# RoPE on one core: splitting the first load around the small inputs, and issuing half of the stores from GpSimd

## Chip, cores, metric

One core of a Trainium2 chip. The metric is the device time of one execution in microseconds (us). The kernel before takes 85.66 us (median of three runs, 85.59 to 85.97).

## The reference

```python
x: float32 (8, 8, 1024, 64); freqs: (32,); positions: int (1024,); scale = 0.5
angles = np.outer(positions * scale, freqs)
cos, sin = np.cos(angles), np.sin(angles)
x_first, x_second = x[..., :32], x[..., 32:]
out = concat([x_first * cos - x_second * sin,
              x_first * sin + x_second * cos], axis=-1).astype(np.float32)
```

16.8 MB are read and 16.8 MB are written.

## The kernel before

The data is cut into eight units of 2 MB, each 128 partitions of 16 KB. Unit 0 is loaded as it is by SyncE and cast to half precision on ScalarE. Units 1 to 7 are loaded by GpSimd, whose transfers cast on the way. VectorE builds the angles from positions and frequencies, ScalarE takes sine and cosine. Then each unit takes four VectorE instructions, a cast back on ScalarE, and a store.

```python
BUF_O = 4
...
    X0f = xin.tile([P, N], FP32, name="X0f")
    nc.sync.dma_start(out=X0f, in_=xv[0])
    pos_i64 = consts.tile([HP, K], positions.dtype)
    nc.scalar.dma_start(out=pos_i64, in_=positions.rearrange("(q k) -> q k", k=K))
    freq_row = consts.tile([1, half], FP32)
    nc.scalar.dma_start(out=freq_row, in_=freqs[None, :])
    ...
    load(1)                       # nc.gpsimd.dma_start(out=X[u], in_=xv[u]), casts
    ...
    for u in range(2, NU):
        load(u)
    ...                           # angles, sinT, cosT; ScalarE casts X0f into X[0]
    for u in (1, 0, *range(2, NU)):
        ps = prods.tile([P, K, 2, half], FP16, tag="ps")
        pin(nc.vector.tensor_tensor(out=ps, in0=X[u], in1=sin_b, op=ALU.mult))
        pin(nc.vector.tensor_tensor(out=X[u], in0=X[u], in1=cos_b, op=ALU.mult))
        ...                       # subtract into the first halves, add into the second
        OUT = xout.tile([P, N], FP32, tag="O")      # four buffers
        pin(nc.scalar.copy(out=OUT, in_=X[u].rearrange("p k h j -> p (k h j)")))
        nc.sync.dma_start(out=ov[u], in_=OUT)
```

## Time and profile before

| | kernel before |
|---|---|
| median time, span of the profiled run | 85.66 us, 83.9 us |
| frequencies land, first rotation starts | 7.82, 17.19 us |
| last store issued, landed on its last DMA engine | 76.43, 82.68 us |
| from the last landing to the end of the span | 1.20 us |
| busy: VectorE, ScalarE | 62.6, 37.4 us |

The span is shorter than the time by a constant 1.8 us; differences can be compared. "Landing" is the arrival of a completion record; a large transfer here runs on 16 DMA engines, each of which leaves one, and the last of them counts. The lines of the page, of the chain of waits and of the windows that carry the argument are in the prediction. "The hole" below is the short stretch, around 77 us, in which the DMA engines have finished the seventh store and the last one has only just been issued.

### The profile page before, as it was taken

What the parts mean: (1) busy time and instruction counts of PE and PEld (TensorE: products, weight loads), DVE (VectorE), ACT (ScalarE), POOL (GpSimd) and SP (SyncE); (2) the same over time, 40 slices, a digit from 0 to 9 for tenths busy, and PEclk for the clock granted to TensorE, in tenths of its full rate; (3) what the DMA queues carried; (4) which work ended last, traced back from release to release, by engine and by line L of the source; (5) the groups of instructions that cost most, each with busy time, mean ns of one, the idle gap of its engine ahead of it and who ended that gap; (6) DMA issues with size and microseconds to landing.
All of it is one profiled execution on the core that took longest, in us unless ns stands there. A gap on an engine that the chain in (4) does not pass through costs nothing.

```text
span 83.9 us, 151 instructions
## 1 busy us (share of the span) xinstructions
PE 1.1 (1%) x4; PEld 0.9 (1%) x4; DVE 62.6 (75%) x40; ACT 37.4 (45%) x12; POOL 4.5 (5%) x13
## 2 busy tenths in 40 slices
PE   0002300000000000000000000000000000000000
PEld 0002200000000000000000000000000000000000
DVE  0010699889999999999999999999999999600000
ACT  1400000799749309608905921950880591294000
POOL 5960000000000000000000000000000000000000
DMA  3599999999999999999999999999999999998890
GB/s 78 207 402 328 289 207 219 215 211 223 203 230 203 231 191 238 313 336 305 313 348 324 313 313 277 426 438 438 438 430 414 445 414 430 438 430 375 375 500 0
DMA packets 2338, 26.22 MB, mean 313 GB/s; under 512 B 274, under 2 KB 290, under 8 KB 290
## 3 DMA queue, kind: packets, MB, share of 16 engines
q1 hardware_dynamic: 1296, 18.87, 53.6%
q0 software_dynamic: 1008, 7.34, 42.7%
q10 hardware_dynamic: 34, 0.01, 0.2%
HBM read 16.79 MB, written 16.78 MB: 400 GB/s over the span
## 4 chain that ended last, share of the span: by engine, by line
DVE 72%; DMA 8%; ACT 7%; DVEq 1%; PE 1%; issue 1%; ACTq 1%
DVE X L136 22%; DVE ps L135 21%; DVE X L137 12%; DVE X L140 9%; DMA freq_row<-in_freqs_dram 8%; ACT OUT L144 4%; DVE r L116 3%; DVE y L107 3%; ACT sinT L120 2%; DVE m L114 1%; DVEq L176 1%; PE cfreq L92 1%; PE pos_ps L100 1%; ACTq L64 0%; DVE posf L104 0%
## 5 line engine op out<-in xcount | busy, mean ns | idle before, releaser
L144 ACT CAST OUT<-X 128x4096 f32<-128x4096 f16 x8 | 28.8, 3605 | 25.0 <-DVE X L140 25.0
L135 DVE TENSOR_TENSOR ps<-X,sinT 128x4096 f16<-128x4096 f16 x8 | 18.3, 2284 | 0.7 <-ACT sinT L120 0.7
L136 DVE TENSOR_TENSOR X<-X,cosT 128x4096 f16<-128x4096 f16 x8 | 18.3, 2292 | 0.3
L137 DVE TENSOR_TENSOR X<-X,ps 128x2048 f16<-128x2048 f16 x8 | 9.8, 1224 | 0.3
L140 DVE TENSOR_TENSOR X<-ps,X 128x2048 f16<-128x2048 f16 x8 | 9.7, 1217 | 0.0
L120 ACT ACTIVATE sinT<-r 128x2048 f16<-128x2048 f32 x1 | 1.9, 1910 | 12.2 <-DVE r L116 12.2
L71 POOL DMA_DIRECT2D X<-in_x_dram x7 | 3.9, 567 | 0.8 <-POOLq L162 0.8
L127 ACT CAST X<-X0f 128x4096 f16<-128x4096 f32 x1 | 3.6, 3587 | 0.0
L104 DVE COPY posf<-pos_ps 128x64 f32<-128x64 f32 x1 | 0.2, 225 | 4.0 <-PE pos_ps L100 4.0
L95 DVE CAST pos_row<-pos_i 16x64 f32<-16x64 int32 x1 | 0.2, 241 | 3.9 <-DMA pos_i<-in_positions_dram 3.9
L116 DVE SCALAR_TENSOR_TENSOR r<-m,y 128x2048 f32<-128x2048 f32 x1 | 2.3, 2292 | 0.0
L107 DVE TENSOR_TENSOR y<-posf,cfreq 128x2048 f32<-128x2048 f32 x1 | 2.3, 2286 | 0.0
L120 ACT ACT_TABLE_LOAD x1 | 1.3, 1283 | 1.7 <-issue 1.7
L126 ACT ACTIVATE cosT<-ra,quarter 128x2048 f16<-128x2048 f32 x1 | 2.0, 1985 | 0.0
L114 DVE TENSOR_SCALAR m<-y 128x2048 f32<-128x2048 f32 x1 | 1.2, 1227 | 0.0
L122 DVE TENSOR_SCALAR ra<-r 128x2048 int32<-128x2048 int32 x1 | 1.2, 1226 | 0.0
L88 DVE MEMSET coef<- 1x128 f32 x1 | 0.2, 165 | 0.8 <-PEq L162 0.8
L92 PE MATMUL cfreq<-freq_row,coef 1*128 1x32 f32 x2 | 0.6, 392 | 8.0 <-DMA freq_row<-in_freqs_dram 8.0
L100 PE MATMUL pos_ps<-pos_row,sel 16*128 16x64 f32 x2 | 0.7, 432 | 0.0
L92 PEld LDWEIGHTS cfreq<-freq_row,coef 1*128 1x128 f32 x2 | 0.5, 308 | 7.9 <-issue 7.9
L100 PEld LDWEIGHTS pos_ps<-pos_row,sel 16*128 16x128 f32 x2 | 0.5, 328 | 0.0
L77 POOL TENSOR_SCALAR_AFFINE_SELECT sel<-sel 16x128 f32<-16x128 f32 x1 | 0.3, 332 | 0.1
(6 smaller groups left out, 0.7 us busy)
## 6 DMA issues: line engine op xcount, KB each, us to landing
out_dram<-OUT SPq DMA_DIRECT2D x8, 2048.0 KB, 14.3
X<-in_x_dram POOLq DMA_DIRECT2D x7, 1024.0 KB, 24.5
X0f<-in_x_dram SPq DMA_DIRECT2D x1, 2048.0 KB, 10.2
pos_i<-in_positions_dram ACTq DMA_DIRECT2D x1, 8.0 KB, 4.1
freq_row<-in_freqs_dram ACTq DMA_DIRECT2D x1, 0.1 KB
```

The source lines that it names most:

```text
L71: nc.gpsimd.dma_start(out=X[u].rearrange("p k h j -> p (k h j)"), in_=xv[u])
L100: nc.tensor.matmul(out=pos_ps, lhsT=sel.rearrange("q a b -> q (a b)"), rhs=pos_row, start=True, stop=True)
L107: pin(nc.vector.tensor_tensor(out=y, in0=posf.unsqueeze(2).broadcast_to((P, K, half)), in1=cfreq.unsqueeze(1).broadcast_to((P, K, half)), ...
L114: pin(nc.vector.tensor_scalar(out=m, in0=y, scalar1=_MAGIC, scalar2=None, op0=ALU.add))
L116: pin(nc.vector.scalar_tensor_tensor(out=r, in0=m, scalar=_MAGIC, in1=y, op0=ALU.subtract, op1=ALU.subtract))
L120: pin(nc.scalar.activation(out=sinT, in_=r, func=AF.Sin, bias=0.0, scale=-_TWO_PI_DN))
L127: pin(nc.scalar.copy(out=X[0].rearrange("p k h j -> p (k h j)"), in_=X0f))
L135: pin(nc.vector.tensor_tensor(out=ps, in0=X[u], in1=sin_b, op=ALU.mult))
L136: pin(nc.vector.tensor_tensor(out=X[u], in0=X[u], in1=cos_b, op=ALU.mult))
L137: pin(nc.vector.tensor_tensor(out=X[u][:, :, 0, :], in0=X[u][:, :, 0, :], in1=ps[:, :, 1, :], op=ALU.subtract))
L140: pin(nc.vector.tensor_tensor(out=X[u][:, :, 1, :], in0=ps[:, :, 0, :], in1=X[u][:, :, 1, :], op=ALU.add))
L144: pin(nc.scalar.copy(out=OUT, in_=X[u].rearrange("p k h j -> p (k h j)")))
```

## The change

Its intent: to have the frequencies sooner, so that VectorE starts sooner; and to let the loads run first, by putting the first four stores into the same queue behind them.

```diff
-    nc.sync.dma_start(out=X0f, in_=xv[0])
+    pin = tc.keep_in_program_order
+    nc.sync.dma_start(out=X0f[:, : N // 2], in_=xv[0][:, : N // 2])
...
-    nc.scalar.dma_start(out=pos_i64, ...)
+    pin(nc.scalar.dma_start(out=pos_i64, ...))
-    nc.scalar.dma_start(out=freq_row, in_=freqs[None, :])
+    pin(nc.scalar.dma_start(out=freq_row, in_=freqs[None, :]))
+    pin(nc.scalar.dma_start(out=X0f[:, N // 2 :], in_=xv[0][:, N // 2 :]))
...
-    for u in (1, 0, *range(2, NU)):
+    for i, u in enumerate((1, 2, 0, *range(3, NU))):
...
-        nc.sync.dma_start(out=ov[u], in_=OUT)
+        (nc.gpsimd if i < NU // 2 else nc.sync).dma_start(out=ov[u], in_=OUT)
```

More of the change, by code (lines that the diff above doesn't have):

```diff
@@ L60 @@
     X0f = xin.tile([P, N], FP32, name="X0f")
-    nc.sync.dma_start(out=X0f, in_=xv[0])
+    pin = tc.keep_in_program_order
+    nc.sync.dma_start(out=X0f[:, : N // 2], in_=xv[0][:, : N // 2])
     pos_i64 = consts.tile([HP, K], positions.dtype)
-    nc.scalar.dma_start(out=pos_i64, in_=positions.rearrange("(q k) -> q k", k=K))
+    pin(nc.scalar.dma_start(out=pos_i64, in_=positions.rearrange("(q k) -> q k", k=K)))
     freq_row = consts.tile([1, half], FP32)
-    nc.scalar.dma_start(out=freq_row, in_=freqs[None, :])
+    pin(nc.scalar.dma_start(out=freq_row, in_=freqs[None, :]))
+    pin(nc.scalar.dma_start(out=X0f[:, N // 2 :], in_=xv[0][:, N // 2 :]))
     X = [xin.tile([P, K, 2, half], FP16, name=f"X{u}") for u in range(NU)]
@@ L82 @@
         load(u)
-    pin = tc.keep_in_program_order
     coef = consts.tile([1, P], FP32)
```

## The prediction

> **What bounds the kernel now.** I read the page first, for who is busy and what the chain of waits says. The chain ends in VectorE work:
>
> ```profile
> DVE 72%; DMA 8%; ACT 7%; DVEq 1%; PE 1%; issue 1%; ACTq 1%
> ```
>
> In order of time, the chain (the second view; columns are start, length, what) has these joints:
>
> ```profile
> 1.19 6.64 DMA freq_row<-in_freqs_dram
> ...
> 7.96 0.60 PE cfreq L92 x2
> 8.56 0.49 PE pos_ps L100 x2
> ...
> 9.08 0.23 DVE posf L104
> ...
> 17.19 2.30 DVE ps L135
> ...
> 72.80 3.60 ACT OUT L144
> ```
>
> So the 128-byte frequency row holds everything up until 7.82 us. From there to the first rotation is fixed work: 17.19 - 7.82 = 9.37 us. Then eight units of 6.92 us on VectorE (17.19 to 24.19, 31.11 and so on, no gap), a 3.60 us cast, and the last store is issued at 76.43. This view alone says: bring the frequencies earlier, and the end comes earlier by as much.
>
> The page's rows of forty slices say otherwise:
>
> ```profile
> DVE  0010699889999999999999999999999999600000
> ...
> DMA  3599999999999999999999999999999999998890
> ...
> HBM read 16.79 MB, written 16.78 MB: 400 GB/s over the span
> ```
>
> DMA is at 90% or more from the third slice almost to the end, longer than VectorE is. The third view, busy time by window, with DMA share and GB/s in the last two columns, tells whether this is real saturation:
>
> ```profile
> 0.00:1.70 1.70, 0.00 (x0) 0.00 (x0) 0.17 (x2) 0.00 (x0) 0.68 (x5) 1.00 0.00 0
> 1.70:3.70 2.00, 0.00 (x0) 0.00 (x0) 0.00 (x0) 1.28 (x1) 1.91 (x6) 1.00 0.85 233
> 3.70:5.70 2.00, 0.00 (x0) 0.00 (x0) 0.24 (x1) 0.00 (x0) 1.93 (x4) 1.00 0.99 418
> 20.00:28.00 8.00, 0.00 (x0) 0.00 (x0) 7.93 (x5) 6.15 (x2) 0.00 (x0) 1.00 1.04 217
> 34.50:54.00 19.50, 0.00 (x0) 0.00 (x0) 19.33 (x12) 9.56 (x4) 0.00 (x0) 1.00 1.02 325
> 56.00:76.00 20.00, 0.00 (x0) 0.00 (x0) 16.55 (x11) 10.41 (x3) 0.00 (x0) 1.00 1.01 433
> 76.00:77.50 1.50, 0.00 (x0) 0.00 (x0) 0.00 (x0) 0.41 (x1) 0.00 (x0) 1.00 0.82 350
> 77.50:78.50 1.00, 0.00 (x0) 0.00 (x0) 0.00 (x0) 0.00 (x0) 0.00 (x0) 1.00 0.77 328
> 78.50:82.40 3.90, 0.00 (x0) 0.00 (x0) 0.00 (x0) 0.00 (x0) 0.00 (x0) 1.00 0.92 387
> 82.40:83.90 1.50, 0.00 (x0) 0.00 (x0) 0.00 (x0) 0.00 (x0) 0.00 (x0) 1.00 0.00 0
> ```
>
> GB/s counts bytes at the destination, and a casting load writes half of what it reads: 217 is 434 GB/s of reading. The mixed stretch at 325 is half 434 of writing and half 217. The rate is thus one and the same, about 433 GB/s, for loads, stores and both. All 33.57 MB at 433 GB/s take 77.5 us of the 83.9 us span. What is left is 1.7 us before the first packet, about 0.9 us lost in 1.70 to 3.70 (233 instead of 418 for 2 us), the weak second around 77 to 78, and 1.2 us after the last landing.
>
> The records of landings settle it. The last engine's parts of stores 3 to 7 land at 63.00, 67.88, 72.72, 77.56 and 82.68 us: 4.88, 4.84, 4.84 and 5.12 apart, while the casts come 6.92 apart. Stores were queued up and drained at DMA speed. Only the last, issued at 76.43 just before the sixth had drained, found a small hole: 5.12 - 4.86 = 0.26 us. The kernel is bound by the DMA engines, and the VectorE chain has nearly caught up with them at the very end. The chain of waits names VectorE only because it follows the last store's own release.
>
> **What the Trainium skill says.** "DMA: Bandwidth & Descriptors", section "Where 436 GB/s comes from", gives 435 GB/s for the ports of the 16 engines, and says that between HBM and SBUF about 358 binds instead. This trace shows 433 in one direction, so here the first figure is the limit. The same page, "Issuing engines are not separate DMA queues", says that it doesn't matter to the transfer which engine issues it. The trace agrees for loads: mixed pairs of a GpSimd load and a SyncE store take 9.8 us, like two stores. Its "Queues, rings and completion order" says each DMA engine takes turns among queues, packet by packet. That agrees too (after 32 us loads and stores alternate), but a newcomer waits longer than one turn: store 0 was issued at 27.93 and its packets begin at about 31.8, and the frequency packet, issued at 1.19, moves at 6.25. "SBUF — State Buffer", section "Who interferes with whom", warns that VectorE can keep GpSimd from writing descriptors only in its two-port modes, not in tensor_tensor. During the stores VectorE runs only tensor_tensor, so I expect no harm; the trace of before has no GpSimd issue at that time to show it.
>
> **The change part by part.** No byte and no engine instruction is added or removed; one load becomes two.
>
> *Half of unit 0 behind the frequencies.* Ahead of the frequency packet there are now 8 packets of 8 KB per DMA engine on the SyncE queue, not 8 of 16 KB. A 16 KB packet takes 0.617 us at this stage, so half takes about 0.31. The frequency packet was served after some 4 packets[...] (2.5 us of its wait); half of that is 1.25 us saved. Its completion packet came at 7.48, 1.2 us later, behind two other packets; with an 8 KB one among them it would be about 0.9. Together about 1.6 to 2.4 us: I put the row's landing at 5.8 us (5.0 to 6.5) and the first rotation at 5.8 + 9.37 = 15.2. Unit 1, landed at 13.43 before, needs the same 4 MB ahead of it moved and is in time. Last cast done at 15.2 + 8 x 6.92 + 0.2 + 3.6 = 74.4, which is 2 us earlier.
>
> What it is worth at the end: only the hole of 0.26 us, since the DMA backlog then covers the last issue. At 74.4 store 6 is still draining (to 77.5).
>
> *Start of the DMA.* First packets were slow (1.0 to 1.7 us against 0.617), then met the positions. That latency remains. Smaller packets can make it a little better or worse; I take 0 +- 0.4 us.
>
> *Stores from GpSimd behind its loads.* They line up in the same rings, so loads run unshared to about 18.3 + 5 x 4.87 = 42.6 us, and stores 0, 1, 2 land near 47.5, 52.4 and 57.3. The buffers: there are four, so the fifth cast waits for store 0. It wants to start at 15.2 + 5 x 6.92 + 0.1 = 49.9. That is 2.4 us to spare; the sixth wants 56.8 against 52.4. Store 3 and SyncE's store 4 share from about 57, landing near 67, against a wanted 70.7 for the eighth cast. No new wait. The DMA never runs dry, as three stores are ready when loads end. Mixed pairs at 9.80 against 2 x 4.86 cost 0.08 us per pair, two pairs or so disappear: -0.1 us.
>
> *Unit order 1, 2, 0.* Unit 2 landed at 18.3 and is needed at 22.1. Unit 0's cast by ScalarE was done at 22.54 before, ahead of its use anyway. Worth 0; it only makes room for an earlier start and for half of unit 0 landing later.
>
> Sum: 85.66 - 0.26 - 0.1 +- 0.4 = 85.3 us.
>
> **The rivals.** (a) The chain of waits is the truth and 2 us come off: 83.7, faster by 2.3%. For it: the chain, and SyncE waiting for each cast before its store. Against it: stores landing 4.86 us apart and 433 GB/s with no pause; 2 us would need a DMA rate that no window shows. (b) The stores from GpSimd cost something: slower packets, or a full buffer. Load packets from GpSimd took 0.625 us against 0.611 for the SyncE stores alone; if that belongs to the issuer, 4 x 8 packets x 0.014 = 0.45 us more, so 85.7. If store 0 landed only after 50, the fifth cast would stall; a stall of x us reaches the end only beyond the 2 us of slack. A long one would make 87 or more. (c) The start: two hardware queues fill the engines sooner and recover most of the 0.9 us: 84.5.
>
> **Range and chances.** 85.3 is the sum. Of (c) most goes into the lower end, 84.5; (b) with the spread of the runs before (85.59 to 85.97) makes the upper end 85.9. Faster by over 2% means below 83.95, 1.35 us below my sum, where only (a) or all gains together reach: 6%. Slower by over 2% means above 87.37, only with a stall or starved descriptors: 3%. Within: 91%.
>
> **What would show it.** Right: frequencies landing near 5.8 and the first rotation near 15.2; the last cast near 74.4, yet the last store landing at 82.2 to 82.6; loads unshared to 42 to 43; DMA share near 1 from 4 to 81 us with no weak second at 77; the last store taking about 8 us instead of 6.25. Wrong: an idle stretch of ScalarE before its fifth cast ended by a store; a DMA window below 0.9 in the middle; GpSimd store packets clearly longer than 0.611; or an end that moves as much as the first rotation does, which would make the VectorE chain the bound after all.

## The result, and the profile after

The changed kernel takes 84.69 us (median of four runs, 84.42 to 84.86) against 85.63 for the kernel before beside it. The ratio is 0.9878, 95% interval 0.9841 to 0.9915. Ratios here are the mean time of one kernel's fast runs over the mean of the other's fast runs of the same rounds, so they are not quite the ratios of the medians quoted. The time lies in the predicted range and in the predicted class (within 2%), but the gain is 0.94 us by the medians (1.03 when it was measured again beside `after_again`) where 0.36 was predicted.

The chain of waits of the changed kernel (start, length, what):

```profile
1.18 4.71 DMA freq_row<-in_freqs_dram
...
15.24 2.30 DVE ps L136
...
70.86 3.60 ACT OUT L145
```

The frequencies land at 5.88 us, not 7.82. The first rotation and the last cast are 1.95 us earlier, and the last store is issued at 74.49. The end of the span moved by 0.79 us only (83.88 to 83.09; the profiled run of the changed kernel is the slowest of its four, 84.86 us). The two rows of forty slices from the page of the changed kernel:

```profile
DVE  0005999699999999999999999999999999000000
...
DMA  2799999999999999999999999999999999999990
```

VectorE's row ends a slice earlier and DMA's doesn't. By windows (DMA share and GB/s last), the changed kernel:

```profile
28.00:34.00 6.00, 0.00 (x0) 0.00 (x0) 5.93 (x5) 3.61 (x1) 0.53 (x1) 1.00 1.04 217
34.00:39.00 5.00, 0.00 (x0) 0.00 (x0) 4.96 (x4) 2.74 (x1) 0.00 (x0) 1.00 1.02 213
39.00:42.00 3.00, 0.00 (x0) 0.00 (x0) 2.97 (x3) 0.87 (x1) 0.53 (x1) 1.00 0.99 175
43.00:53.00 10.00, 0.00 (x0) 0.00 (x0) 9.90 (x7) 6.51 (x2) 0.53 (x1) 1.00 1.01 433
56.00:76.00 20.00, 0.00 (x0) 0.00 (x0) 14.64 (x9) 10.81 (x3) 0.00 (x0) 1.00 1.01 432
76.00:77.50 1.50, 0.00 (x0) 0.00 (x0) 0.00 (x0) 0.00 (x0) 0.00 (x0) 1.00 1.10 470
77.50:78.50 1.00, 0.00 (x0) 0.00 (x0) 0.00 (x0) 0.00 (x0) 0.00 (x0) 1.00 0.84 360
```

Loads now run alone to 43.24 us (217 GB/s at the destination is 434 of reading), then the stores of GpSimd at 433. The weak stretch around 77 us is gone: before, 350 and 328 GB/s in the last two of these windows; now 470 and 360, which is 426 on average. One stretch that I had not foreseen is busy yet slow, 39 to 42 us at 175; more of it below.

The rest lies behind the last landing, where no engine works. One view of the kernel's closing line (SyncE's instructions of it from 82.5 to 83.1 us in the kernel before, and from 82.1 to 82.35 in the changed one; the count comes after the x, then the durations in ns, then the first and last start in us):

```profile
L176 SPq EVENT_SEMAPHORE  x6: 28/28/28, 82.7 to 83.0; - x6
```

```profile
L177 SPq EVENT_SEMAPHORE  x1: 28/28/28, 82.2 to 82.2; - x1
```

At the end SyncE goes through a fixed list of semaphores, one instruction each, and waits for each in turn; the starts are 0.06 us apart. The transfers of the hardware queues take eight semaphores in rotation. Before, there were 3 loads and 8 stores, 11 such transfers, so the last store held the third of the list, and five more instructions came after its landing: 5 x 0.06 = 0.30 us. In the changed kernel there are 4 + 4 = 8, and the last store holds the last one. From last landing to end: 1.20 us before, 0.90 after. Together with 0.49 us by which the last landing itself moved (82.68 to 82.19), that is the 0.79 us.

### The profile page after: what moved, and what is told of

Its sections match the earlier page's. It is cut to its first block, busy times and chain, and to the rows that moved or that the text cites. A ratio compares the mean times of both kernels' runs of the same rounds, so it can differ in the third digit from the quotient of the medians.

```text
span 83.1 us, 154 instructions
## 1 busy us (share of the span) xinstructions
PE 1.1 (1%) x4; PEld 0.9 (1%) x4; DVE 62.5 (75%) x40; ACT 37.4 (45%) x12; POOL 6.7 (8%) x17
## 4 chain that ended last, share of the span: by engine, by line
DVE 72%; ACT 7%; DMA 6%; DVEq 1%; PE 1%; issue 1%; ACTq 1%
DVE X L137 22%; DVE ps L136 21%; DVE X L138 12%; DVE X L141 10%; DMA freq_row<-in_freqs_dram 6%; ACT OUT L145 4%; DVE r L117 3%; DVE y L108 3%; ACT sinT L121 2%; DVE m L115 1%; DVEq L177 1%; PE cfreq L93 1%; PE pos_ps L101 1%; ACTq L66 0%; DVE posf L105 0%
## 5 line engine op out<-in xcount | busy, mean ns | idle before, releaser
L146 POOL DMA_DIRECT2D out_dram<-OUT x4 | 2.1, 534 | 39.7 <-ACT OUT L145 39.7
```

The source lines that it names most:

```text
L146: (nc.gpsimd if i < NU // 2 else nc.sync).dma_start(out=ov[u], in_=OUT)
```

## The experiments

The theory: DMA bound; the gain is the hole before the last store, a smoother passage of loads and stores, and the list of waits at the end. Rival 1: the VectorE chain is the bound and its earlier start gives the gain. Rival 2: unmixing loads and stores gives all of it. All runs gave a right result, except one that is wrong. The table has one profiled run of each kernel; times and ratios come from six runs each against eleven of the kernel before on the same chip (four and four in the first two rows). These elevens had medians of 85.45 us (rows `half_only` to `before_last_lane`), 85.61 (`after_no_add` to `after_early_write`) and 85.59 (the last three), so a gain is read from the ratio and not against the 85.63 of the first row.

| kernel | median us | ratio | first rotation | last issue | 7th store landed | last landing | landing to end |
|---|---|---|---|---|---|---|---|
| before | 85.63 | 1 | 17.19 | 76.43 | 77.56 | 82.68 | 1.20 |
| changed | 84.69 | 0.9878 | 15.24 | 74.49 | 77.35 | 82.19 | 0.90 |
| half_only | 85.24 | 0.9954 | 14.90 | 74.15 | 77.47 | 82.32 | 1.13 |
| stores_only | 85.36 | 0.9953 | 16.44 | 75.69 | 77.07 | 81.94 | 0.90 |
| order_only | 85.65 | 0.9996 | 17.12 | 76.37 | 77.35 | 82.63 | 1.19 |
| before_last_lane | 85.32 | 0.9963 | 17.14 | 76.38 | 77.35 | 82.63 | 0.89 |
| after_no_add | 84.59 | 0.9880 | 15.17 | 73.60 | 77.11 | 81.96 | 0.89 |
| after_late2 | 85.83 | 1.0027 | 17.65 | 76.90 | 77.28 | 83.15 | 0.90 |
| after_first_lane | 85.08 | 0.9938 | 15.10 | 74.34 | 77.17 | 82.01 | 1.33 |
| after_early_write | 85.01 | 0.9927 | 15.08 | 74.33 | 77.13 | 81.97 | 1.33 |
| after_again | 84.56 | 0.9882 | 15.19 | 74.44 | 77.10 | 81.95 | 0.89 |
| half_last_lane | 85.04 | 0.9937 | 15.49 | 74.74 | 77.59 | 82.44 | 0.90 |
| after_early_write_pool | 84.76 | 0.9902 | 15.04 | 74.30 | 77.38 | 82.20 | 0.91 |

### One part at a time

half_only has the first half of the change's diff (unit 0 split, positions and frequencies between the halves) and nothing else.

> Only unit 0's load is split, with positions and frequencies ahead of the second half; all stores stay on SyncE, order stays 1, 0, 2. Theory (DMA bound, three small gains): first rotation near 15.2 us and last store issued near 74.5, but only the hole before the last store goes (0.26 us) and the last store's semaphore is one place later in the final list of waits (4 waits after it, not 5, 0.06 us): 0.3 us faster, 85.3. Rival 1 (the VectorE chain is the bound, half of the 1.95 us reaches the end): 0.9 us or more faster, 84.7 or less. Rival 2 (all comes from unmixing loads and stores): 0.

85.24 us, 0.9954 (0.9922 to 0.9986), which is 0.39 us by the ratio. The first rotation starts 2.3 us earlier, yet that is all. The windows of half_only at the hole:

```profile
75.50:76.50 1.00, 0.00 (x0) 0.00 (x0) 0.00 (x0) 0.00 (x0) 0.00 (x0) 1.00 0.99 426
76.50:77.50 1.00, 0.00 (x0) 0.00 (x0) 0.00 (x0) 0.00 (x0) 0.00 (x0) 1.00 1.08 459
```

It is closed (before, 361 GB/s in the second of these windows and 328 in the next one, which has 393 here), and the wait list is shortened by 0.07 us. Rivals 1 and 2 both miss.

stores_only has the last line of the diff alone.

```diff
-    for u in (1, 0, *range(2, NU)):
+    for i, u in enumerate((1, 0, *range(2, NU))):
-        nc.sync.dma_start(out=ov[u], in_=OUT)
+        (nc.gpsimd if i < NU // 2 else nc.sync).dma_start(out=ov[u], in_=OUT)
```

> Only the first four stores go to GpSimd; unit 0 whole, order 1, 0, 2. Theory: DMA has about 0.2 to 0.3 us less to do by the end, but the last store is issued at 76.43 as before and lands 6.2 us later, so that shows as a larger hole; the last store's semaphore comes last but at most one in the final list of waits: 0.3 us faster, 85.3. Rival 1 (VectorE chain): 0. Rival 2 (unmixing): 0.9 us faster, 84.7.

85.36 us, 0.9953 (0.9915 to 0.9992). Its profiled run is its fastest (84.62), in which the frequencies happened to land at 7.08, so its row in the table is about 0.7 us better than its median. The windows of stores_only at the same place:

```profile
75.50:76.50 1.00, 0.00 (x0) 0.00 (x0) 0.00 (x0) 0.16 (x1) 0.00 (x0) 1.00 0.28 115
76.50:77.50 1.00, 0.00 (x0) 0.00 (x0) 0.00 (x0) 0.00 (x0) 0.00 (x0) 1.00 1.22 524
```

Here the seventh store had landed earlier (77.07 against 77.56), so the engines had caught up, and they were 28% busy until the last store came, whose issue hangs on VectorE. What the stores gain is lost in a larger hole as long as VectorE isn't earlier too. That is why the two halves belong together. The 0.40 us are hardly the stores' own: with seven transfers of the hardware queues, the last store also comes last in the list of waits, and before_last_lane below, which changes nothing but that place, has 85.32 us in the same call.

order_only has the new order of units alone.

```diff
-    for u in (1, 0, *range(2, NU)):
+    for u in (1, 2, 0, *range(3, NU)):
```

> Only the unit order 1, 2, 0, 3 to 7. All theories: 0, within 0.2 us; unit 2 landed at 18.3 us and is needed at 24.2, no wait of VectorE appears.

0.9996 (0.996 to 1.0032): nothing, as predicted.

### The list of waits at the end

before_last_lane adds five tiny loads that nothing reads to the kernel before, so that 3 + 5 + 8 = 16 transfers rotate through the eight semaphores and the last store holds the last.

```diff
+    for i in range(5):
+        spare = consts.tile([1, half], FP32, name=f"spare{i}")
+        nc.sync.dma_start(out=spare, in_=freqs[None, :])
```

> The kernel before with five 128-byte loads to spare tiles behind unit 0's load on SyncE, which nothing reads; they shift the rotation of eight semaphores so that the last store's semaphore is the last that SyncE waits for at the end. Theory: time from the last landing to the end of the span falls from 1.20 to 0.90 us, 0.3 us faster, 85.3, with the last landing unchanged at 82.7. Rivals: the 0.3 us is chance, and the time stays at 85.65.

85.32 us, 0.9963 (0.993 to 0.9995), 0.32 us by the ratio (0.13 by the medians, of which those of the kernel before scatter over 0.8 us); last landing within 0.05 us, 0.89 us to the end. after_first_lane does the opposite to the changed kernel: the same loop with `range(1)`, so that the last store holds the first of eight.

> The changed kernel with one 128-byte load to a spare tile behind the first half of unit 0, so that the last store's semaphore is the first of eight in the final list of waits. Theory: 7 waits of 0.06 us follow the last landing, 0.9 us becomes 1.3: 0.4 us slower, 85.1. Rival (the list costs nothing, the gain of the changed kernel lies elsewhere): 84.7.

85.08 us, 0.9938 against 0.9878 and 0.9882 for the changed kernel in two other calls, 0.5 us slower; 1.33 us from landing to end, seven waits more. Its view of SyncE's closing line, 81.9 to 82.7 us:

```profile
L180 SPq EVENT_SEMAPHORE  x8: 28/28/28, 82.0 to 82.5; - x8
```

Rotating the place by loads of 128 bytes moves the stretch behind the last landing both ways by the expected 0.3 and 0.4 us, and the time by 0.3 and 0.4 to 0.5. This term is shown.

### Is VectorE the bound?

after_no_add takes the last addition of each unit away from the changed kernel. Its output is wrong, which doesn't matter for the time.

```diff
-        pin(nc.vector.tensor_tensor(
-            out=X[u][:, :, 1, :], in0=ps[:, :, 0, :], in1=X[u][:, :, 1, :], op=ALU.add
-        ))
```

> The changed kernel without the last addition of each unit on VectorE (second halves wrong on purpose): a unit takes 5.78 us there, not 6.92, 9.1 us less in all. Theory (DMA bound): 84.7 within 0.3, and ScalarE's fifth cast now waits for the first store to land near 48. Rival (VectorE chain bound): 75.6 to 76.

84.59 us, 0.9880 (0.9856 to 0.9904): 9.1 us of VectorE's work are gone, and the time is that of the changed kernel. The page of after_no_add has VectorE at 53.4 us, and its waits name what holds the casts now:

```profile
PE 1.1 (1%) x4; PEld 0.9 (1%) x4; DVE 53.4 (65%) x32; ACT 37.4 (45%) x12; POOL 6.7 (8%) x17
...
ACT OUT L142 <- DMA out_dram<-OUT: 17.0, 4, 6.1
```

In the changed kernel all eight waits of the casts were for VectorE (25.0 us); here the last four wait 17.0 us for stores to free the buffers. The fifth cast was the one for which the prediction reckoned 2.4 us to spare; take VectorE's work away, and it waits. Rival 1 is refuted for the changed kernel in this direction.

after_late2 does the addition of the magic number three times in the changed kernel.

```diff
+    pin(nc.vector.tensor_scalar(out=m, in0=y, scalar1=_MAGIC, scalar2=None, op0=ALU.add))
+    pin(nc.vector.tensor_scalar(out=m, in0=y, scalar1=_MAGIC, scalar2=None, op0=ALU.add))
```

> The changed kernel with the 1.23 us addition of the magic number done three times, so that the first rotation starts 2.5 us later, at 17.7, and the last store is issued near 76.9. Theory: a last store that finds the engines empty lands 6.25 us after its issue, so 83.2 us, 1.0 us later than in the changed kernel: 85.7. Rival (chain): 2.5 us later, 87.1. Rival (DMA alone, no second bound): 0.

85.83 us, 1.0027 (1.0002 to 1.0052). The last store is issued 2.41 us later and lands 0.96 us later, 6.25 us after its issue. Its window:

```profile
76.50:77.50 1.00, 0.00 (x0) 0.00 (x0) 0.00 (x0) 0.37 (x1) 0.00 (x0) 1.00 0.01 0
```

A full microsecond of idle DMA. So the changed kernel has some 1.45 us of slack on VectorE (2.41 - 0.96; 1.26 against the trace of after_again). Beyond it VectorE sets the end.

The same 6.25 us from issue to landing of the last store stand in the kernel before (76.43 to 82.68), and within 0.01 us in order_only, before_last_lane and stores_only. There too the end hung on VectorE's issue, so the kernel before stood on the other side of the same edge. A second sign: in these kernels and in after_late2 the 16 engines' landings of the last store lie within 0.11 to 0.18 us of each other, in the others, where each engine still drains its own backlog, 0.56 to 0.91 us apart.

### What the stores of GpSimd are worth

half_last_lane is half_only with four spare loads (the loop above with `range(4)`), so that it differs from the changed kernel in the stores' issuer and the order of units, but not in the place of the last semaphore. after_again is the changed kernel, unaltered, on the same chip.

> Unit 0 split as in the change, all stores on SyncE in the old order, and four 128-byte loads to spare tiles so that the last store's semaphore stands last in the final list of waits. It has two of the three gains without any store on GpSimd. Theory (GpSimd's stores give 0.1 to 0.15 us by unmixing, and the semaphore's place): last landing 82.2 to 82.4 and 0.90 us to the end, 0.1 to 0.2 us slower than the changed kernel, 84.8 to 84.9. Rival (the stores behind the loads are worth 0.4 us by themselves): 85.1.

> The changed kernel itself, to stand beside the two others on one chip: 84.7 us, ratio 0.988 within 0.003, last landing near 82.1, 0.90 us from there to the end.

85.04 us and 0.9937 (0.9912 to 0.9961) against 84.56 and 0.9882 (0.9856 to 0.9907). The rival was right here about the time: with the stores on GpSimd it is 0.48 us shorter by the medians, not 0.1 to 0.2. Not all of that is theirs. In the traces of the two, the last landings differ by 0.49 us, but 0.20 of that was there when the fourth of GpSimd's loads landed (28.06 against 27.86), before any store moved data, and the slow packets of the next section took 0.53 us in the one trace and 0.28 in the other.

More traces separate the terms. Take the seventh store's landing, as the mean of its 16 records, and subtract the fourth load's and the time that load packets after 20 us took beyond 0.625 us (their sum, divided by the 16 engines). The rest is 48.85 to 48.91 us in the five kernels with all stores on SyncE and 48.69 to 48.76 in the six with four on GpSimd (without an early write): 0.15 us less, with no overlap. That is what the stores' place is worth to the DMA engines; the prediction reckoned 0.1. The slow packets don't follow the issuer: 0.25 to 0.74 us in the five, 0.09 to 0.64 in the six, and 0.47 and 0.28 in two traces of the changed kernel itself. The fourth load's mean is about 0.1 us earlier where unit 0 is split (27.54 to 27.72) than where it isn't (27.69 to 27.78). What of the pair's 0.48 us lies beyond 0.15 us belongs to the slow packets and the start in the two traces; whether it does so in all runs is not shown.

### The slow packets ahead of the first store

In the changed kernel 30 load packets, most of them between 39.2 and 42 us, took over 0.64 and up to 1.15 us where 0.625 is usual, just ahead of the first store in the queue. In the kernel before the like happens at 30 to 33 us, when its first store comes up. The fifth and sixth of GpSimd's loads of the changed kernel land 4.85 us apart, the sixth and seventh 5.51. I took it for the cost of the first write to the output, and wrote 512 bytes per partition there early. after_early_write does so from SyncE, at the place of the last unit:

```diff
+    warm = consts.tile([P, 128], FP32)
+    pin(nc.vector.memset(warm, 0.0))
+    nc.sync.dma_start(out=ov[NU - 1][:, :128], in_=warm)
```

> As the run before, but the small transfer is a store of 512 bytes per partition of zeros to the place of the last unit in the output, which the last store writes over at the end. In both kernels load packets take near 1 us instead of 0.625 just as the first store comes up (30 to 33 us before, 39 to 42 after), which costs about 0.65 us in the changed kernel. Theory (the first write to the output is slow, whoever makes it): the slow packets are gone from 39 to 42 us and the last landing is 0.4 to 0.65 us earlier than in the run with the spare load: 84.5 to 84.7. Rival (it comes with the turn from loads to stores, or with 2 MB stores only): slow packets stay, 85.1.

85.01 us, 0.9927, against 85.08 and 0.9938 for the run with the spare load: no difference that the intervals (0.99 to 0.9954, 0.9913 to 0.9962) separate. Slow packets are fewer (14), but stores_only has 9 and after_again 24 without any early write. The two landings are 5.30 us apart rather than 5.50, but not 4.87; at the start the second of GpSimd's loads landed 0.22 us later. after_early_write_pool writes from GpSimd, behind its first load, to the place of the unit that is stored first (`nc.gpsimd.dma_start(out=ov[1][:, :128], in_=warm)`).

> The changed kernel with a store of 512 bytes per partition of zeros, from GpSimd behind its first load, to the place of unit 1, whose store comes first and writes over it; the last store's semaphore stays last. Theory (each place or queue is slow at its first write): slow load packets appear near 13 us instead of 39 to 42, and the gap between the landings of the sixth and the seventh load falls from 5.5 to 4.9 us; the end moves by 0 to 0.5 us, 84.2 to 84.7. Rival (the turn from loads to a stream of stores is slow, whatever was written before): still 5.3 to 5.6 us, 84.7.

84.76 us, 0.9902 (0.9874 to 0.9931), not faster than after_again; the landings are 5.37 us apart, and the slow stretch is where it was. The window of after_early_write_pool:

```profile
39.00:42.00 3.00, 0.00 (x0) 0.00 (x0) 2.97 (x3) 0.67 (x1) 0.53 (x1) 1.00 0.95 161
```

My theory of a slow first write falls, at least for small writes like these. The slow stretch comes with the first full store, 0.4 to 0.65 us between the two landings in each of the kernels of this section, and what makes it, and why it varies so much, stays open. No version here beats the changed kernel.

## Why the prediction was right, and where a size was off

**DMA binds, VectorE doesn't.** Right for the changed kernel, by after_no_add: 9.1 us less VectorE work, no change. For the kernel before, the prediction said that the chain of waits names VectorE only because it follows the last store's own release. That is too strong: its end did wait for VectorE's issue (6.25 us, as above). What was right, and decided the result, is how little that is worth: of 1.94 us by which the last store was issued earlier, the hole of 0.26 us came off before the DMA engines set the end.

**The earlier start.** Frequencies predicted at 5.8, landed at 5.88; first rotation 15.2, was 15.24; last store issued at 74.4, was 74.49; the last store took 7.70 us, about 8 predicted. Worth only the hole of 0.26 us: half_only gained 0.39, of which 0.07 is the list of waits. Right. The working behind the 5.8 (four packets of unit 0 ahead of the frequencies, two others ahead of their completion) is not shown: the packet records don't name the engine.

**No new wait.** The fifth cast started at 50.09, as VectorE released it, with the first store landed at 48.16. Right, though the margin was 1.9 us, not 2.4, since the slow packets held the first store back. Store packets issued by GpSimd took 0.611 us like those of SyncE; rival (b) had thought of 0.625, and falls. Descriptors (the entries that GpSimd writes for the DMA engines) were not starved, as the prediction expected: GpSimd issued each store in 0.53 to 0.54 us while VectorE was busy all the time.

**Unit order.** 0, and order_only shows 0.

**Unmixing, "-0.1 us", and the start, "0 +- 0.4".** Nearly right: 0.15 and about 0.1 us by the averages over the engines.

**The DMA time that is left over.** The prediction sets 77.5 us of moving against a span of 83.9 and lists what is left; its list makes 4.1 us of 6.4. Among the missing are the slow packets at 30 to 33 us, 0.74 us, the largest loss in the middle of the kernel, which its windows (20 to 28, then 34.5 on) step over.

**What the sum lacked.** This is the step where the size was off. The sum ended at the last landing and took the 1.2 us behind it as fixed. Of these 0.30 us depended on which semaphore the last store holds, and the change moved it there by accident of counting: eight hardware transfers instead of eleven. The terms are then 0.26 (hole; 0.43 in the traces of order_only and before_last_lane) + 0.15 (unmixing) + 0.1 (start) + 0.30 (wait list) = 0.8, against 0.94 and 1.03 us by the times, whose intervals reach down to 0.73 and 0.80. The two profiled spans differ by 0.79, but that is no independent check of each term: slow packets that vary from trace to trace, and engines that end 0.91 us apart in the changed kernel, are in it too.

**The range.** It held partly by luck. Its lower end was kept for rival (c), a quicker start, which came to 0.1 us; what brought the time there was the list of waits, which no part of the prediction has.

## What to carry to other kernels

Ask of a chain of waits whether the last transfer was waiting for its issue or for its predecessors: stores landing at even steps of bytes over rate say the second, whatever the chain names; a last store that takes no longer than it does on idle engines (6.25 us here), with all its engines landing together, says the first. Two bounds that nearly meet have to be moved together: the stores alone gave nothing beyond the list of waits and left the engines idle, and the earlier start alone ran into the engines after 0.26 us. And look behind the last landing: a kernel that ends with a list of waits pays for each that stands behind its last transfer.

## What the Trainium skill lacked or had wrong

- "DMA: Bandwidth & Descriptors", "Where 436 GB/s comes from": its sentence that about 358 GB/s binds between HBM and SBUF is too wide. The page's own table of measured loads ("Measured (HBM→SBUF, 128 partitions, SWDGE, issued from GpSimd)") has 425 for one core alone and keeps 358 for two cores that both stream. One core alone moved 433 here, in loads, in stores and in both.
- The same page, "Issuing engines are not separate DMA queues": issuing from several engines saves only issue time. The rate was indeed the same, but which queue a store stands in decides its place behind the loads, and that was worth 0.15 us of DMA time here; the section has nothing on that.
- The same page, "Queues, rings and completion order": turns are taken packet by packet, but the first store that joined the loads waited some 4 us (issued at 27.93, first packet at 31.94 in the kernel before; 3.8 to 4.0 in all five kernels with the stores on SyncE). The page gives no figure for that.
- No page that I looked in has the slow load packets ahead of the first store: up to 1.2 us instead of 0.625 in the changed kernel and its variants, 0.1 to 0.75 us in all by the trace, and two small early writes did not remove them.
- Nor did I find one with the closing list of waits: 0.06 us for each semaphore behind that of the last transfer, 0 to 0.42 us by its place.
